# Operand-sum stores on SyncE's queue, weight sums spread over all gate steps, and another order of places at both ends of the down stage

## The chip, the cores and the metric

The kernel runs on one core of one Trainium2 chip. A core has TensorE (PE, the matmuls), VectorE (DVE), ScalarE (ACT), GpSimd (POOL) and SyncE (SP). Each has an instruction queue of its own that is worked off in order; SP issues DMAs only, and ACT issues DMAs between its own computations. The metric is the time of one execution on the device in microseconds, as the median of three runs; lower is better.

## What is computed

Two transformer-like blocks on 2048 tokens (and 16 meta tokens) with 1024 features. The change sits in the feed-forward part (FFN) of the first block, whose hidden size is 2816:

```
n2 = rmsnorm(h, norm2_g[i])
ff = jax.nn.silu(n2 @ w_gate[i]) * (n2 @ w_up[i])
h = h + ff @ w_down[i]
...
return second_block(first_block(...), ...)
```

Ahead of it the first block has a state-space mixer and a pooling mixer with an output projection; the second block has chunk-banded attention, gated linear attention and a gate on a per-layer embedding. Everything is float32 to the reference.

## The kernel before

**Precision.** Every float32 product is made of three matmuls of a rounded type: operand x is split into a high part (ACT copies it, `wh`, `xh`) and a low part (DVE or POOL subtracts the high part, `wl`, `xl`), and TensorE adds high by high, high by low and low by high. Splitting (`halves`, `split_in`) is thus work of ACT and of DVE or POOL for every operand.

**FFN.** The tokens are worked in two halves of 1024. For each half there is a gate stage (`gu_half`, `down_start` at its end) and a down stage (`down`). Both use a Strassen-like scheme: 2 by 2 blocks with 7 products in place of 8, so operands are sums and differences of blocks.

- *Gate stage*: 22 steps `j`, each of 7 products of 12 matmuls in the order 1, 2, 6, 5, 7, 3, 4 (line 1091). The operands of a step are made by `gu_w` (line 1033) one step ahead: `wr` (gate weights) and `wru` (up weights) are loaded, POOL and DVE make sums `wru`, `sq`, `wr`, and these are split into `wh`/`wl`, `wth`/`wtl`, `wsh`/`wsl`. ACT also takes the products out of PSUM (`t`, `raw`). Each pair of steps gives 7 hidden operands for the down stage: products in `raw`, `ha`, `hb`, `hc`, some with a POOL subtraction (`less`). `put` stores each to DRAM (`hd_d`): 77 stores of 256 KB in a half.
- *Weight sums*: 4 of the 7 left operands of the down stage are sums of blocks of `w_down`. `down_sums` (line 1186) makes them in gate half 0: 44 tiles, each with two loads (`sd<-in_w_down`), four POOL subtractions or additions of 128x128 (176 in all) and one store to `sd_d`. A step advances it twice.
- *Down stage*: 77 places of 12 matmuls (line 1316). `dn_load` loads the two operands, `dn_split` splits them: every third place (`dn_s % 3 == 1`) into the single tiles `wth`, `wtl`, `hc`, `hd`, the others into the doubly buffered `wh`, `wl`. The tile `hc` is the one that held a hidden operand in the gate stage. Place 0 and its loads begin inside the last gate step. Near the end of down half 0 (`n == 75`), `gu_prime` loads the first weights of gate half 1.

Beside this run background generators (`bg_step`): in gate half 0 `bias_table` (stores `eb_d<-e`, on ACT), in gate half 1 `norm` (stores `h_d<-nh`, on ACT).

**Order.** A framework takes the program text, and puts each engine's instructions into a queue order by priorities and data flow; semaphores do the rest. So the order on an engine can differ from the program text, and an instruction that waits holds back all that is behind it on its engine. `load` issues a DMA on SP, `store` on ACT:

```
def load(self, o, i):
    self.nc.sync.dma_start(out=o, in_=i)
def store(self, o, i):
    self.nc.scalar.dma_start(out=o, in_=i)
```

Of the kernel before, what the change touches and what calls it, by code (L numbers as in the profile page):

```python
# [10 lines left out]
ALU = mybir.AluOpType  # L11
# [24 lines left out]
class Build:  # L36
# [1034 lines left out]
        put(7, 4, *self.split_in(ru, self.wp, [128, KT, 128], 2, "", None))  # L1071
        yield 1

    def gu_prime(self):

        self.gu_js = [i // 2 + i % 2 * (NFF // 2) for i in range(NFF)]
        self.gu_raws = [self.gu_load(0, False), None]
        self.gw_steps = self.gu_w(0)
        next(self.gw_steps)

    def gu_half(self, half):

        def product(ps, p, first, last):
            hi, lo = w[p]
            x = self.xg[p]
            ks = range(4)
            for k in ks:
                for n, (l_, r_) in enumerate(((hi, 0), (hi, 1), (lo, 0))):  # L1090
                    self.pe.matmul(ps, lhsT=l_[:, k], rhs=x[k][r_], start=(first and k == n == 0),  # L1091
                                   stop=(k == 3 and n == 2), skip_group_check=True)

        def bank(name):
            return self.ps.tile([128, 512], F32, tag="ps", name=name, bufs=8)

        def gated(g):
            th = self.tmp("raw", 4)
            self.fn(th, g, AF.Tanh, scale=0.5)
            self.stt(th, th, 1.0, g, ALU.add, ALU.mult)  # L1100
            return th

        def keep(name):
            return self.fp.tile([128, 512], F32, tag=name, name=name, bufs=1)

        def less(o, x, y):
            self.tt(o, x, y, ALU.subtract, eng=self.pool)

        def put(p, x):
            self.store(self.hd_d[half, p - 1, jj], x)  # L1110

        sums = iter(()) if half else self.down_sums()
        for j in range(NFF):
            jj, late = j // 2, j % 2
            w = self.gw
            next(sums, None)
            nw = self.gu_w(j + 1) if j + 1 < NFF else iter(())
            pa, pb = bank("pa"), bank("pb")
            product(pa, 1, True, False)
            s1 = self.tmp("t", 2)  # L1120
            self.fn(s1, pa, AF.Copy)
            product(pb, 2, True, True)
            self.tt(s1, pb, s1, ALU.add)
            h0 = gated(s1)
            next(nw, None)
            next(nw, None)
            if j == NFF - 1:
                self.down_start(half)
                self.dn_load()
                self.dn_load()  # L1130
                self.dn_split()
            product(pa, 6, False, False)
            s2 = self.tmp("t", 2)
            self.fn(s2, pa, AF.Copy)
            pc = bank("pc")
            product(pc, 5, True, False)
            p5 = self.tmp("raw", 4)
            self.fn(p5, pc, AF.Copy)
            next(nw, None)
            product(pa, 7, False, False)  # L1140
            self.tt(p5, pa, p5, ALU.add)
            product(pc, 3, False, True)
            self.tt(s2, pc, s2, ALU.add)
            h1 = gated(s2)
            next(nw, None)

            if late:
                self.tt(h1, h1, p5, ALU.mult)
                put(3, h1)
                less(hb, h1, hb)  # L1150
                put(7, hb)
                less(hc, h1, hc)
                put(6, hc)
            else:
                hb = keep("hb")
                self.tt(hb, h1, p5, ALU.mult)
            next(sums, None)
            if j == 0 and self.r2_todo:
                self.mix_r2(*self.r2_todo.pop())
            if j % 2:  # L1160
                self.bg_step()
            product(pa, 4, False, True)
            if late:
                self.tt(h0, pa, h0, ALU.mult)
                put(2, h0)
                less(ha, h0, hc)
                put(4, ha)
            else:
                ha, hc = keep("ha"), keep("hc")
                self.tt(ha, pa, h0, ALU.mult)  # L1170
                put(1, ha)
                less(hc, hb, ha)
                put(5, hc)
            next(nw, None)
            self.bg_step()

# [9 lines left out]
    def down_sums(self):  # L1186

        wd, h = self.a["w_down"], NFF // 2

        def fetch(j, m):  # L1190
            t = self.fp.tile([128, 4, 128], F32, tag="ls", name="sd", bufs=3)
            self.load(t[:, 0:2], wd[j][:, m::4])
            self.load(t[:, 2:4], wd[j + h][:, m::4])
            return t

        todo = [(j, m) for j in range(h) for m in range(4)]
        nxt = fetch(*todo[0])
        for i, (j, m) in enumerate(todo):
            t = nxt
            if i + 1 < len(todo):  # L1200
                nxt = fetch(*todo[i + 1])
            for o, x, y, op in ((1, 0, 1, ALU.subtract), (3, 3, 1, ALU.subtract), (0, 0, 3, ALU.add), (2, 2, 3, ALU.subtract)):
                self.tt(t[:, o], t[:, x], t[:, y], op, eng=self.pool)
            self.store(self.sd_d[:, j, :, m * 128:(m + 1) * 128].rearrange("s p c -> p s c"), t)
            yield 1

    def down_start(self, half):
# [23 lines left out]
    def dn_split(self):  # L1231

        if not self.dn_raw or self.dn_s == len(self.dn):
            return
        w, x = self.dn_raw.pop(0)
        if self.dn_s % 3 == 1:
            wh, wl, xh, xl = (self.fp.tile([128, 512], F32R, tag=t, name=t, bufs=1) for t in ("wth", "wtl", "hc", "hd"))
        else:
            h, l_ = (self.wp.tile([128, 2, 512], F32R, tag=t, name=t, bufs=2) for t in ("wh", "wl"))
            wh, xh, wl, xl = h[:, 0], h[:, 1], l_[:, 0], l_[:, 1]  # L1240
        self.halves((wh, wl), w)
        self.halves((xh, xl), x)
        self.dn_s += 1
        self.dn_ops.append((wh, wl, xh, xl))

    def down(self, half):
# [9 lines left out]
        h1, kept, sums, hold, post = [], [[None] * KT for _ in range(2)], {}, {}, []  # L1256
# [35 lines left out]
        def done(p, m):  # L1292

            ps = (pa if p in (1, 6, 7, 4) else pb)[m]
            if p in (1, 6, 5):
                if m == 0:
                    places(p)
                self.fn(hold[p][m], ps, AF.Copy)
            elif p == 4:
                out(ps)  # L1300
            else:
                x = hold[{2: 1, 7: 5, 3: 6}[p]][m]
                self.tt(x, ps, x, ALU.add)
                out(x)
# [1 line left out]
        for _ in range(2):  # L1306
            fetch()
        for n, (p, j) in enumerate(self.dn):
            self.dn_split()
            self.dn_load()  # L1310
            wh, wl, xh, xl = self.dn_ops.pop(0)
            ps = pa if p in (1, 6, 7, 4) else pb
            for m in range(4):
                c = slice(m * 128, m * 128 + 128)
                for i, (l_, r_) in enumerate(((wh, xh), (wh, xl), (wl, xh))):
                    self.pe.matmul(ps[m], lhsT=l_[:, c], rhs=r_, start=(p in (1, 2, 5) and j == i == 0),
                                   stop=(j == NFF // 2 - 1 and i == 2), skip_group_check=True)
            if post:
                done(*post.pop(0))
            if j == NFF // 2 - 1:  # L1320
                post += [(p, m) for m in range(4)]
            if n % 4 == 1:
                self.bg_step()
            if n == 75:
                if half:
                    self.w_all = self.weights("proj")
                    self.w_next.append(self.get_w(0))
                else:
                    self.gu_prime()
                    next(self.gw_steps)  # L1330
        while post:
            done(*post.pop(0))
# [720 lines left out]
```

## Time and profile before

| | |
|---|---|
| Median of 3 runs | 3585.68 us (3585.02 to 3585.87) |
| The profiled execution | 3588.34 us, its span 3586.4 us |
| Mean granted TensorE clock | 0.957 |
| Busy, PE / DVE / ACT / POOL | 91% / 63% / 45% / 41% |
| DMA traffic | 573.95 MB, 160 GB/s |
| Gate half 0 / down half 0 | about 679 to 1146 us / 1157 to 1377 us |
| Gate half 1 / down half 1 | about 1377 to 1852 us / 1862 to 2078 us |

The span is the time between the first and the last instruction that the profiler saw; the time of an execution is a little longer. The granted clock is the share of full speed that TensorE was allowed. A busy share is an average over the whole span: a stage must be looked at by itself.

### The profile page before, as it was taken

What the parts mean: (1) busy time and instruction counts of PE and PEld (TensorE: products, weight loads), DVE (VectorE), ACT (ScalarE), POOL (GpSimd) and SP (SyncE); (2) the same over time, 40 slices, a digit from 0 to 9 for tenths busy, and PEclk for the clock granted to TensorE, in tenths of its full rate; (3) what the DMA queues carried; (4) which work ended last, traced back from release to release, by engine and by line L of the source; (5) the groups of instructions that cost most, each with busy time, mean ns of one, the idle gap of its engine ahead of it and who ended that gap; (6) DMA issues with size and microseconds to landing.
All of it is one profiled execution on the core that took longest, in us unless ns stands there. A gap on an engine that the chain in (4) does not pass through costs nothing. (4 is left out here: it accounts for less than half of the span.)

```text
span 3586.4 us, 46677 instructions
## 1 busy us (share of the span) xinstructions
PE 3273.8 (91%) x15874; PEld 2712.4 (76%) x15874; DVE 2253.7 (63%) x3697; ACT 1608.9 (45%) x2906; POOL 1469.1 (41%) x1234
## 2 busy tenths in 40 slices
PE   7897788789998998999989989999999999979897
PEld 7776666667887787777878777898888987867676
DVE  7776556754556756776555672335665446888774
ACT  5344533323333543344344442335665445766643
POOL 1265544798543203554520142232222235354534
PEclk8898899899999999999999999999999999989999
DMA  9634276676233664354356534565464565545341
GB/s 243 150 109 105 80 222 198 183 233 191 100 109 123 218 217 155 126 173 153 108 204 191 176 132 165 174 184 178 155 175 145 165 186 165 166 146 157 121 164 54
DMA packets 406342, 573.95 MB, mean 160 GB/s; under 512 B 90668, under 2 KB 222276, under 8 KB 406104
## 3 DMA queue, kind: packets, MB, share of 16 engines
q1 hardware_dynamic: 270144, 419.23, 39.7%
q10 hardware_dynamic: 135960, 151.75, 12.4%
q8 instruction: 125, 2.05, 0.2%
q14 instruction: 113, 0.93, 0.1%
HBM read 409.04 MB, written 151.71 MB: 156 GB/s over the span
## 5 line engine op out<-in xcount | busy, mean ns | idle before, releaser
L44 POOL TENSOR_TENSOR wl<-wr,wh 128x1024 fp32r<-128x1024 f32 (+1 forms) x147 | 372.7, 2537 | 314.7 <-ACT wh L54 295.2
L54 ACT ACTIVATE wh<-wr 128x1024 fp32r<-128x1024 f32 (+3 forms) x303 | 272.7, 902 | 341.6 <-PE pt L159 75.8
L158 PE MATMUL pt<-xh,wh 128*128 128x512 f32 x896 | 362.3, 405 | 16.3 <-ACT wh L54 8.2
L160 PE MATMUL pt<-xh,wl 128*128 128x512 f32 x896 | 358.8, 401 | 4.3 <-POOL wl L44 4.3
L159 PE MATMUL pt<-xl,wh 128*128 128x512 f32 x896 | 359.1, 401 | 0.2 <-DVE xl L44 0.2
L48 POOL TENSOR_SCALAR P<-P,rsm 128x640 f32<-128x640 f32 (+4 forms) x128 | 103.4, 808 | 346.7 <-DVE rsm L1628 285.2
L1091 PE MATMUL pa<-xh,wh 128*128 128x512 f32 x528 | 214.6, 407 | 24.2 <-ACT t L54 20.3
L44 DVE TENSOR_TENSOR wl<-wr,wh 128x512 fp32r<-128x512 f32 (+2 forms) x156 | 150.3, 964 | 106.0 <-ACT wh L54 105.6
L1091 PE MATMUL pa<-xh,wl 128*128 128x512 f32 x528 | 209.5, 402 | 3.7 <-POOL wl L44 3.6
L158 PEld LDWEIGHTS pt<-xh,wh 128*128 128x128 f32 x896 | 171.1, 191 | 54.3 <-ACT wh L54 9.6
L1091 PE MATMUL pa<-xl,wh 128*128 128x512 f32 x528 | 211.8, 401 | 0.0
L44 POOL TENSOR_TENSOR s<-s,sq 128x512 f32<-128x512 f32 x56 | 87.9, 1569 | 285.6 <-ACT sq L54 284.4
L160 PEld LDWEIGHTS pt<-xh,wl 128*128 128x128 f32 x896 | 170.7, 191 | 41.9 <-POOL wl L44 6.2
L159 PEld LDWEIGHTS pt<-xl,wh 128*128 128x128 f32 x896 | 171.3, 191 | 35.6 <-DVE xl L44 0.7
L1623 DVE CUSTOM_DVE_ANT_0 P<-s,bias 128x640 f32<-128x640 f32 (+4 forms) x128 | 94.6, 739 | 111.5 <-PE s L1618 71.2
L1488 PE MATMUL pv<-wh,xh 128*128 128x256 f32 (+1 forms) x512 | 148.0, 292 | 5.5 <-ACT wh L54 3.9
L1489 PE MATMUL pv<-wl,xh 128*128 128x256 f32 (+1 forms) x512 | 147.6, 289 | 0.7 <-POOL wl L44 0.7
L1490 PE MATMUL pv<-wh,xl 128*128 128x256 f32 (+1 forms) x512 | 147.0, 288 | 0.0
L1091 PE MATMUL pc<-xh,wsh 128*128 128x512 f32 x352 | 139.1, 395 | 6.0 <-ACT wsh L54 3.2
L1091 PEld LDWEIGHTS pa<-xh,wh 128*128 128x128 f32 x528 | 101.5, 192 | 54.2 <-ACT t L54 24.6
L54 ACT ACTIVATE wsh<-wr 128x1024 fp32r<-128x1024 f32 x44 | 46.6, 1060 | 211.9 <-PE pc L1091 149.8
L1091 PE MATMUL pc<-xl,wsh 128*128 128x512 f32 x352 | 139.0, 395 | 0.0
(516 smaller groups left out, 9898.2 us busy)
## 6 DMA issues: line engine op xcount, KB each, us to landing
raw<-hd_d SPq DMA_DIRECT2D x150, 256.0 KB, 3.6
wr<-in_w_out SPq DMA_DIRECT2D x56, 512.0 KB, 4.5
wr<-in_w_in SPq DMA_DIRECT2D x44, 512.0 KB, 3.8
wru<-in_w_up SPq DMA_DIRECT2D x44, 512.0 KB, 3.6
wr<-in_w_gate SPq DMA_DIRECT2D x44, 512.0 KB, 3.4
wr<-sd_d SPq DMA_DIRECT2D x88, 256.0 KB, 2.9
wr<-in_w_down SPq DMA_DIRECT2D x66, 256.0 KB, 3.7
nh<-h_d SPq DMA_DIRECT2D x64, 256.0 KB, 3.8
```

What stands on the lines that cost most here:

```text
L44: return (eng or self.dve).tensor_tensor(out=o, in0=x, in1=y, op=op)
L48: (eng or self.dve).tensor_scalar(out=o, in0=x, scalar1=s1, scalar2=s2, op0=op0, **kw)
L54: return self.act.activation(out=o, in_=x, func=func, **kw)
L158: self.pe.matmul(ps, lhsT=hi[k], rhs=xh[k], start=(first and k == 0), stop=False)
L159: self.pe.matmul(ps, lhsT=hi[k], rhs=xl[k], start=False, stop=False)
L160: self.pe.matmul(ps, lhsT=lo[k], rhs=xh[k], start=False, stop=(last and k == n - 1))
L1091: self.pe.matmul(ps, lhsT=l_[:, k], rhs=x[k][r_], start=(first and k == n == 0), stop=(k == 3 and n == 2), skip_group_check=True)
L1488: self.pe.matmul(pt, lhsT=xh, rhs=whi[:, k % 4], start=(k == 0), stop=False)
L1489: self.pe.matmul(pt, lhsT=xh, rhs=wlo[:, k % 4], start=False, stop=False)
L1490: self.pe.matmul(pt, lhsT=xl, rhs=whi[:, k % 4], start=False, stop=(k == KT - 1))
L1623: self.dve.tensor_tensor_reduce(out=v3(P[:, 0:w]), in0=sp[:, 0:np_, 0:n], in1=v3(bias[:, 640 - w:640]), scale=1.0, scalar=3e38, op0=ALU.ad ...
```

## The change

Three things, all in the FFN:

1. `put` and the store of `down_sums` go through `load`: 154 stores to `hd_d` and 44 to `sd_d` are issued by SP in place of ACT.
2. The two advances of `down_sums` move from two places inside a gate step to its end, and are placed after the step's last `less` on POOL, so that 8 of the 176 POOL operations fall in each of the 22 steps.
3. In the down stage the single tiles are taken at `dn_s % 3 == 2` (and at 73 and 76 near the end), `dn_split` and `dn_load` come behind a place's matmuls in the text; and at the end of down half 0 `gu_prime` loads both weights at `n == 73`, with the first three steps of `gu_w(0)` at 74, 75 and 76.

```
-    def gu_prime(self):
+    def gu_prime(self, both=False):
...
-        self.gu_raws = [self.gu_load(0, False), None]
+        self.gu_raws = [self.gu_load(0, False), self.gu_load(0, True) if both else None]
         self.gw_steps = self.gu_w(0)
-        next(self.gw_steps)
+        if not both:
+            next(self.gw_steps)
...
         def less(o, x, y):
-            self.tt(o, x, y, ALU.subtract, eng=self.pool)
+            self.less = self.tt(o, x, y, ALU.subtract, eng=self.pool)
 
         def put(p, x):
-            self.store(self.hd_d[half, p - 1, jj], x)
+            self.load(self.hd_d[half, p - 1, jj], x)
...
             w = self.gw
-            next(sums, None)
             nw = self.gu_w(j + 1) if j + 1 < NFF else iter(())
...
                 self.tt(hb, h1, p5, ALU.mult)
-            next(sums, None)
             if j == 0 and self.r2_todo:
...
                 put(5, hc)
+            with self.tc.issue_after(self.less.ins):
+                next(sums, None)
+                next(sums, None)
             next(nw, None)
...
-            self.store(self.sd_d[:, j, :, m * 128:(m + 1) * 128].rearrange("s p c -> p s c"), t)
+            self.load(self.sd_d[:, j, :, m * 128:(m + 1) * 128].rearrange("s p c -> p s c"), t)
...
-        if self.dn_s % 3 == 1:
+        if self.dn_s in (73, 76) or self.dn_s < 72 and self.dn_s % 3 == 2:
...
         for n, (p, j) in enumerate(self.dn):
-            self.dn_split()
-            self.dn_load()
             wh, wl, xh, xl = self.dn_ops.pop(0)
...
                                    stop=(j == NFF // 2 - 1 and i == 2), skip_group_check=True)
+            self.dn_split()
+            self.dn_load()
...
-            if n == 75:
-                if half:
-                    self.w_all = self.weights("proj")
-                    self.w_next.append(self.get_w(0))
+            if half and n == 75:
+                self.w_all = self.weights("proj")
+                self.w_next.append(self.get_w(0))
+            if not half and n >= 73:
+                if n == 73:
+                    self.gu_prime(True)
                 else:
-                    self.gu_prime()
                     next(self.gw_steps)
```

Three places show how the instructions move.

ACT in a gate step of half 0, from the split of the up weights (`wh<-wru`) to the split of the next operand (`wth<-sq`) and the product out of PSUM (`t<-pa`). Before:

```order
L54 ACTIVATE wh<-wru 128x1024
L54 ACTIVATE raw<-t 128x512
L54 ACTIVATE wh<-wr 128x1024
L60 DMA sd_d<-sd 128x4x128
L60 DMA hd_d<-ha 128x512
L60 DMA sd_d<-sd 128x4x128
L54 ACTIVATE wth<-sq 128x512
L54 ACTIVATE t<-pa 128x512
```

The same stretch of ACT's queue, of the changed kernel:

```order
L54 ACTIVATE wh<-wru 128x1024
L54 ACTIVATE wh<-wr 128x1024
L54 ACTIVATE raw<-t 128x512
L60 DMA eb_d<-e 128x256
L60 DMA eb_d<-e 128x512
L54 ACTIVATE wth<-sq 128x512
L54 ACTIVATE t<-pa 128x512
```

The stores of sums and of hidden operands no longer stand ahead of `wth` and `t`; the two of the bias table still do in the first steps.

TensorE from the last gate step (line 1091, in the changed kernel 1092) to the first places of the down stage (line 1316). Before, product 4 and then place 1, which is in the single tiles:

```order
L1091 MATMUL pa<-xh,wl 128x512
L1091 MATMUL pa<-xh,wh 128x512
L1091 MATMUL pa<-xl,wh 128x512
L1091 MATMUL pa<-xh,wl 128x512
L1316 MATMUL pa<-hc,wth 128x512 x4
```

Of the changed kernel, product 3, eleven matmuls of place 1, product 4 (its twelve, of which the inner ones read alike), the last of place 1, and place 2:

```order
L1092 MATMUL pc<-xl,wsh 128x512
L1092 MATMUL pc<-xh,wsl 128x512
L1316 MATMUL pa<-wh 128x512 x4
L1316 MATMUL pa<-wl,wh 128x512
...
L1316 MATMUL pa<-wl,wh 128x512
L1092 MATMUL pa<-xh,wh 128x512
...
L1092 MATMUL pa<-xh,wl 128x512
L1316 MATMUL pa<-wh,wl 128x512
L1316 MATMUL pa<-hc,wth 128x512 x4
```

Place 1 has moved ahead of product 4, and the first place in the tile `hc` is place 2.

DVE from down half 0 to gate half 1: `h` and `st` are the results of the down stage, `sq`, `wr` and `wtl` the operands of the first gate step. Before:

```order
L51 SCALAR_TENSOR_TENSOR h_11405<-pa,h_11405 128x512
...
L51 SCALAR_TENSOR_TENSOR st_10278<-h_11582,v_final_norm_g,st_10278 128x512
L44 TENSOR_TENSOR t<-pb,t 128x512
L51 SCALAR_TENSOR_TENSOR st_10278<-h_11590,v_final_norm_g,st_10278 128x512
L44 TENSOR_TENSOR sq<-wru 128x512
L51 SCALAR_TENSOR_TENSOR raw<-raw,t 128x512
L44 TENSOR_TENSOR wr<-wr,sq 128x512 x2
```

Of the changed kernel:

```order
L44 TENSOR_TENSOR wtl<-wr,wth 128x512
L44 TENSOR_TENSOR sq<-wru 128x512
L44 TENSOR_TENSOR wr<-wr,sq 128x512 x2
L51 SCALAR_TENSOR_TENSOR h_11403<-pa,h_11403 128x512
L51 SCALAR_TENSOR_TENSOR h_11436<-pa,h_11436 128x512
L51 SCALAR_TENSOR_TENSOR st_10278<-h_11403,v_final_norm_g,st_10278 128x512
L44 TENSOR_TENSOR wsl<-wr,wsh 128x1024
L44 TENSOR_TENSOR wtl<-sq,wth 128x512
```

`sq` and `wr` stood behind the four results of the down stage and now stand ahead of them.

## Rows read from the trace of the kernel before

**Rows 1.** The page: busy time, share of the span and instructions of each engine.

```profile
PE 3273.8 (91%) x15874; PEld 2712.4 (76%) x15874; DVE 2253.7 (63%) x3697; ACT 1608.9 (45%) x2906; POOL 1469.1 (41%) x1234
```

**Rows 2.** Stretches: us, busy PE, PEld, DVE, ACT, POOL (count), clock, DMA share, GB/s.

```profile
710.50:890.70 180.20, 162.91 (x674) 127.20 (x673) 92.97 (x111) 49.12 (x69) 158.38 (x184) 0.97 0.71 219
890.70:1124.00 233.30, 233.30 (x1009) 189.17 (x1008) 136.92 (x147) 80.65 (x112) 111.47 (x59) 1.00 0.29 101
...
1376.70:1410.90 34.20, 23.45 (x87) 17.74 (x86) 20.42 (x21) 10.58 (x16) 17.89 (x10) 0.80 0.23 77
1410.90:1610.20 199.30, 185.12 (x768) 146.18 (x767) 151.66 (x155) 82.22 (x115) 102.22 (x56) 0.97 0.44 147
1610.20:1829.80 219.60, 216.37 (x927) 174.75 (x926) 132.95 (x148) 83.61 (x116) 106.31 (x57) 0.99 0.36 124
```

**Rows 3.** PE's waits, 640 to 700: waiting instruction, releaser: us, times, longest.

```profile
PE mo L160 <- POOL wl L44: 4.5, 2, 2.6
PE pa L1091 <- DVE wtl L44: 3.8, 1, 3.8
```

**Rows 4.** PE's waits, 700 to 900.

```profile
PE pa L1091 <- ACT t L54: 11.6, 8, 7.9
```

**Rows 5.** Timeline of ACT in that stretch: start, us, instruction [idle before <-releaser].

```profile
765.84 0.38 ACTq L60 DMA_DIRECT2D sd_d<-sd  x1
...
771.27 0.63 ACT L54 ACTIVATE wth<-sq 128x512 fp32r<-128x512 f32 x1 [8.58 <-DMA sd_d<-sd]
```

**Rows 6.** ACT's waits, 700 to 900.

```profile
ACT t L54 <- POOL sd L44: 13.6, 4, 5.2
...
ACT raw L54 <- DVE e L1549: 6.3, 1, 6.3
```

**Rows 7.** Tile `sd`, POOL's instructions: ns min/median/max, first and last start.

```profile
L44 POOL TENSOR_TENSOR sd<-sd x176: 446/464/1457, 653.5 to 890.0; 128x128 f32<-128x128 f32 x176
```

**Rows 8.** Timeline of DVE, first gate step of half 0.

```profile
686.99 4.50 DVE L44 TENSOR_TENSOR wr<-wr,sq 128x512 f32<-128x512 f32 x2
```

**Rows 9.** PE's waits at the end of gate half 0, 1130 to 1160.

```profile
PE pa L1316 <- ACT hc L54: 10.3, 1, 10.3
```

**Rows 10.** PE's waits at the end of gate half 1, 1851 to 1900.

```profile
PE pa L1316 <- ACT hc L54: 9.9, 1, 9.9
```

**Rows 11.** Timeline of POOL at the end of gate half 0.

```profile
1147.81 1.71 POOL L44 TENSOR_TENSOR hc<-raw,hc 128x512 f32<-128x512 f32 x1
```

**Rows 12.** Timeline of ACT at the end of gate half 0.

```profile
1150.89 0.33 ACTq L60 DMA_DIRECT2D hd_d<-hc  x1
...
1156.04 0.63 ACT L54 ACTIVATE hc<-s 128x512 fp32r<-128x512 f32 x1 [0.75 <-DMA hd_d<-hc]
```

**Rows 13.** A stretch with the columns of rows 2, behind such a pause.

```profile
1862.10:1866.10 4.00, 4.00 (x9) 3.14 (x10) 0.66 (x1) 0.00 (x0) 0.00 (x0) 0.50 0.92 329
```

**Rows 14.** PE's waits at the start of gate half 1, 1380 to 1420.

```profile
PE pa L1091 <- ACT wth L54: 6.7, 1, 6.7
PE pc L1091 <- ACT wsh L54: 3.2, 1, 3.2
```

**Rows 15.** Timeline of DVE there.

```profile
1387.93 1.74 DVE L44 TENSOR_TENSOR sq<-wru 128x512 f32<-128x512 f32 x1
...
1394.77 0.68 DVE L44 TENSOR_TENSOR wr<-wr,sq 128x512 f32<-128x512 f32 x1
```

**Rows 16.** PE's waits in gate half 1, 1420 to 1650.

```profile
PE pa L1091 <- ACT t L54: 11.4, 5, 4.4
```

**Rows 17.** Timeline of ACT in gate half 1, one step.

```profile
1442.68 0.60 ACT L54 ACTIVATE t<-pa 128x512 f32<-128x512 f32 x1 [4.68 <-DVE nh L51]
```

**Rows 18.** The same, another step.

```profile
1490.73 0.63 ACT L54 ACTIVATE wth<-sq 128x512 fp32r<-128x512 f32 x1 [3.86 <-POOL ha L44]
```

**Rows 19.** Timeline of SP in a steady gate step of half 0.

```profile
950.90 0.33 SPq L57 DMA_DIRECT2D wr<-in_w_gate  x1
```

**Rows 20.** Timeline of ACT, the step behind it.

```profile
974.04 1.06 ACT L54 ACTIVATE wh<-wr 128x1024 fp32r<-128x1024 f32 x1 [1.08 <-PE pb L1091]
```

**Rows 21.** The page: DMA issues, their KB and median us to landing.

```profile
wr<-in_w_gate SPq DMA_DIRECT2D x44, 512.0 KB, 3.4
```

## The prediction

> **What bounds the kernel now.** The page comes first: TensorE is busy 91% of the span, the next engine 63% [rows 1]. So almost any gain must come out of TensorE's pauses, and the question is where those are. The table of stretches tells. In steps 9 to 21 of gate half 0 TensorE is busy for all of 233.3 us: 12 steps, so a step without pauses takes 233.3 / 12 = 19.44 us. The same code needs 180.2 us for steps 1 to 8, 34.2 us for step 0 of half 1, 199.3 us for its steps 1 to 9, and 219.6 us for its steps 10 to 20 [rows 2]. The excess over 19.44 us a step is 24.7, 14.8, 24.3 and 5.8 us. In the first of these stretches POOL is busy 158 of 180 us, in the pauseless one 111 of 233: the sums are all worked off early, up to 890 us [rows 7], when the weights' own low parts are also due on POOL.
>
> The views of waits say who ends the pauses. In gate half 0 it is nearly always the copy of a product out of PSUM, `t`, on ACT [rows 4]. ACT is not short of time there (49 of 180 us busy) [rows 2], it stands. The timeline shows how: the store of a weight sum is at the head of ACT's queue, the split `wth` behind it starts after 8.58 us of standing [rows 5], then `t` runs, and TensorE has waited 7.9 us, the longest wait of that group [rows 4]. A store's issue takes 0.4 us; what costs is that it waits on ACT for POOL's result. ACT's own list of waits agrees: `t` 13.6 us behind POOL's `sd` [rows 6].
>
> **The change, part by part.** I number the terms; the sum goes against the profiled execution (3588.34 us), which is 2.7 us above the median of the runs.
>
> 1. *End of the mixer stage and gate step 0.* POOL's sums stood between low parts of weights; TensorE waited 4.5 us for POOL's `wl` and 3.8 us for `wtl` [rows 3]. In front of `wtl` two DVE operations took 4.50 us [rows 8], where one such takes 0.68 [rows 15]: 3.1 us over, beside POOL's sums. The new order has no sum on POOL before the first step's last subtraction. So 4.5 + 3.1, and about 0.9 us of clock (below): **8.5 us**. Bounds 4 (only half of the waits go) and 11 (all of both, with the clock).
>
> 2. *Steps 1 to 8 of half 0*, excess 24.7 us. With neither sums nor hidden operands stored on ACT, what is left there are the stores of the bias table, which wait for DVE's `e` and hold ACT in the first steps: 6.3 us in one row [rows 6]. I keep 5 us for these: **19.7 us**. Bounds 12 (the bias table holds as long twice over) and 24 (all).
>
> 3. *Gate to down, both halves.* TensorE waits 10.3 and 9.9 us for the split `hc` [rows 9, 10]: place 1 is to be split into the tile `hc`, whose hidden operand is made by POOL until 1147.81 + 1.71 = 1149.5, sent from ACT only at 1150.9 and landed at about 1155.3 (1156.04 less the 0.75 of standing); the split runs at 1156.0 [rows 11, 12]. Now place 1 is in other tiles, and its 12 matmuls (12 x 19.44 / 84 = 2.8 us) run before product 4; place 2 is the one that waits. The store can go when POOL is done, so about 1.4 us earlier. 2.8 + 1.4, and a little of the clock: 4.5 us a half, **9 us**. Bounds 6 and 13.
>
> 4. *Down half 0 to gate half 1*, excess 14.8 us. TensorE waits 6.7 us for `wth` and 3.2 us for `wsh` [rows 14]; `wth` needs DVE's `sq`, which runs at 1387.9 behind all results of the down stage [rows 15]. With the weights fetched two places earlier and `sq`, `wr` ahead of those results, both waits should go, and with them clock: **11 us**; 3.8 us stay, for the results' own loads and copies. Bounds 7 and 13.5.
>
> 5. *Steps 1 to 20 of half 1*, excess 24.3 + 5.8 = 30 us. Its waits are for `t` again [rows 16], but of two kinds. In one ACT stands behind a hidden operand's store (3.86 us behind POOL's `ha`) [rows 18]; in the other behind the background norm (4.68 us behind DVE's `nh`) [rows 17], whose stores stay on ACT. By following each long pause back I put a third down to the first kind, half to the second: **10 us** go. Bounds 5 and 13.
>
> 6. *New costs.* Work is moved, not added. The 176 sums (0.464 us each) [rows 7] now fall 8 to a step, 3.7 us of POOL in 19.44 us where POOL is under half busy [rows 2]; the 198 issues on SP, at 0.4 us, are 4 us a step on an engine that does nothing else. From DVE's 4.50 us [rows 8] I take some delay in steps 9 to 21, and the changed rotation of tiles in the down stages is worth nothing to TensorE in either direction that I can see: **-3 us**, bounds -20 (1.5 us in each of 13 steps) and +5.
>
> *The clock* is in the terms: behind a long pause the granted clock is 0.50 for 4 us (1.2 in place of 2.4 GHz) [rows 13], while in a pauseless stretch it is 1.00. Such a spell is 2 us of lost work at most, and goes with the pause.
>
> Sum: 8.5 + 19.7 + 9 + 11 + 10 - 3 = 55.2 us. 3588.3 - 55.2 = 3533.1, less 2.7: **3531 us**. All terms at their upper bounds (74.5 us) give 3511; all at their lower ones (34 - 20 = 14) give 3572.
>
> A rule speaks against terms 2 and 5. The Trainium skill, "DMA: Bandwidth & Descriptors", section "Issuing engines are not separate DMA queues", says that DMAs of all engines run on the same 16 DMA engines, and that another issuing engine saves only the sequencer's time to initiate. Read with 0.4 us for an issue, it makes the move to SP worth little, which is rival A; the 8.58 us [rows 5] speak against this reading, since the sequencer also stands while a store's data isn't ready.
>
> **The rivals.**
>
> *A: the move to SP is worth its issue time only*, because the data or the DMA engines, not ACT's queue, set the pace. Then terms 2 and 5 together give what ten pauses lose in issue, 4 us, and term 3 loses the 1.4 us a half: 8.5 + 4 + 6.5 + 11 - 3 = 27 us, 3559 us. For it: DMA share 0.71 in steps 1 to 8 [rows 2]. Against it: ACT standing behind `sd`, not behind landings [rows 6].
>
> *B: new waits take half.* Where ACT no longer stands for sums it stands for the bias table's and the norm's stores [rows 6, 17], and POOL's sums meet DVE's sums of two tiles [rows 8]. Terms 2, 3, 4, 5 at 10, 4.5, 6 and 3: 8.5 + 23.5 - 3 = 29 us, 3557 us. For it: both kinds of store stay on ACT. The Trainium skill, "SBUF — State Buffer", section "Who interferes with whom", has DVE with two inputs in SBUF and a reading POOL instruction exclude each other; rows 8 agree (4.50 us for two).
>
> *C: slower, through SP's queue.* SP works in order too. A store of a sum now waits at its head for POOL, and the next weights' loads stand behind it. In a steady step the gate weights are sent for at 950.9 and land 3.4 us later, and ACT splits them at 974.0 [rows 19 to 21]: 23.1 - 3.4 = 19.7 us to spare. If SP is held for longer than that in a step, each step waits for a landing: 3.4 us and 2 us of clock, 5.4 us in 18 steps (22 less the first four, whose loads were sent before the stores), 97 us, against 55 gained: 3588.3 + 42 - 2.7 = 3628 us. Against it: a whole step's length is spare, and the sums of a step need only 3.7 us of POOL and come last in it.
>
> **How the numbers follow.** A measurement of this kernel tells about 0.2% (7 us) from no change. The forecast has 0.57, A 0.10, B 0.21, C 0.12. Faster: all of the forecast, 0.09 of A and 0.18 of B, 0.84. Within 0.2%: the weak ends of A, B and C, 0.01, 0.03 and 0.02, 0.06. Slower: 0.10 of C. The range from 3510 to 3572 takes in the sum's bounds, and A and B with them; what is left out is C, some of the edges of the others, 0.2 in all.
>
> **What would show it.** Right: in steps 1 to 8 of half 0 ACT no longer stands behind `sd` or a store of `sd_d`, and the stretch is near 160 us; steps 9 to 21 keep 19.4 to 19.7 us with POOL busier; the pause before the first place in `hc` is 5 to 6 us, not 10; gate step 0 of half 1 takes about 23 us; the waits behind `nh` stay. Wrong: pauses for `wh` or `wl` whose releaser is a landing of `wr` or `wru` (C); steps 9 to 21 longer than 20 us with DVE operations of several us (B); waits for `t` of the old size behind `e` (B), or steps 1 to 8 as long as before though ACT has no stores of sums (A).

## The result, and the profile after

The changed kernel takes 3551.95 us (median of 4 runs, 3551.42 to 3554.38) where the kernel before takes 3585.77 (4 runs): ratio 0.9907, 95% interval 0.9891 to 0.9922. That is 34 us faster, inside the range, where 3531 us was forecast. The direction and most of the places were right; two terms of the sum (1 and 3) brought next to nothing, and the term that brought most (2) did so by another cause than the one given.

The page's busy times of the changed kernel, in the columns of [rows 1]:

```profile
PE 3272.3 (92%) x15874; PEld 2717.1 (76%) x15874; DVE 2268.4 (64%) x3697; ACT 1612.7 (45%) x2906; POOL 1483.5 (42%) x1234
```

TensorE's work is the same; what changed is its pauses, and the clock behind them. The stretches of the changed kernel, in the columns of [rows 2]: steps 1 to 8 of half 0, steps 9 to 20, step 21 with down half 0, step 0 of half 1, its steps 1 to 20, and step 21 with down half 1:

```profile
709.95:873.29 163.34, 157.64 (x673) 127.35 (x672) 103.61 (x112) 55.62 (x75) 114.20 (x104) 0.98 0.55 171
873.30:1106.20 232.90, 232.90 (x1010) 189.30 (x1009) 147.30 (x145) 80.07 (x110) 167.97 (x155) 1.00 0.50 154
1106.17:1361.22 255.05, 238.50 (x1010) 192.15 (x1009) 178.38 (x251) 120.86 (x213) 63.42 (x42) 0.97 0.69 221
1361.22:1382.71 21.49, 19.96 (x86) 15.62 (x85) 19.70 (x19) 8.05 (x13) 14.50 (x8) 1.00 0.39 123
1382.71:1794.32 411.61, 399.27 (x1694) 320.36 (x1692) 284.02 (x306) 167.44 (x233) 212.35 (x113) 0.98 0.40 137
1794.32:2040.38 246.06, 235.77 (x1011) 191.48 (x1010) 152.64 (x220) 116.28 (x203) 31.78 (x17) 0.98 0.64 205
```

The same stretches of the kernel before, where [rows 2] cut them otherwise:

```profile
1124.04:1376.82 252.78, 236.30 (x1009) 192.36 (x1008) 176.62 (x252) 120.74 (x213) 50.12 (x25) 0.97 0.67 215
1410.89:1829.85 418.96, 401.55 (x1694) 320.93 (x1693) 284.66 (x302) 165.88 (x230) 208.54 (x113) 0.98 0.40 135
1829.85:2078.14 248.29, 235.66 (x1011) 191.06 (x1010) 154.28 (x220) 116.75 (x203) 27.82 (x17) 0.97 0.63 203
```

The gain is in steps 1 to 8 (180.2 to 163.3 us, with POOL's share down from 158 of 180 us to 114 of 163) and in step 0 of half 1 (34.1 to 21.5, where the clock stays at 1.00 in place of 0.80). The stretch with the start of down half 0, where a gain was forecast, is 2.3 us longer.

The table sets all kernels of this study side by side, in us, from the starts of the first matmul of each step in the one profiled execution of each. "To step 1" is all that lies ahead of step 1 of half 0, "rest" all behind the down stage of half 1. "Rotation" is the choice of the places that are split into the single tiles, with the order of splits that goes with it. Runs of one kernel, measured together, spread by 3 to 16 us (before: 3574 to 3589 in one such group). Stretches of the same code mostly differ by up to 4 us between profiles, once by 7.5 (steps 1 to 20 of half 1: 419.0 us before, 411.5 with the early fetch alone), so a single difference of that size shows nothing.

| Kernel | to step 1 | 1 to 8 | 9 to 20 | 21, down 0 | 0 of half 1 | 1 to 20 | 21, down 1 | rest | ratio to before (95%) |
|---|---|---|---|---|---|---|---|---|---|
| before | 710.5 | 180.2 | 233.4 | 252.8 | 34.1 | 419.0 | 248.3 | 1508.2 | 1 |
| changed | 709.9 | 163.3 | 232.9 | 255.0 | 21.5 | 411.6 | 246.1 | 1512.0 | 0.9907 (0.9891 to 0.9922) |
| changed, second time | 707.1 | 163.4 | 232.9 | 255.5 | 21.8 | 411.6 | 243.8 | 1510.3 | 0.9919 (0.9899 to 0.9938) |
| stores alone | 712.4 | 180.9 | 233.4 | 246.2 | 34.0 | 411.6 | 249.6 | 1500.7 | 0.9989 (0.9978 to 1.0) |
| sums alone | 707.2 | 163.5 | 232.9 | 251.8 | 33.4 | 415.4 | 246.4 | 1506.7 | 0.9944 (0.9925 to 0.9963) |
| places and fetch alone | 712.1 | 179.7 | 233.4 | 252.2 | 21.5 | 413.5 | 245.8 | 1501.7 | 0.9950 (0.9932 to 0.9967) |
| early fetch alone | 711.6 | 181.0 | 233.4 | 251.5 | 24.9 | 411.5 | 248.9 | 1511.0 | 0.9981 (0.9972 to 0.9991) |
| changed, stores on ACT | 708.7 | 163.6 | 232.9 | 255.1 | 21.4 | 413.6 | 248.6 | 1507.7 | 0.9919 (0.9904 to 0.9933) |
| changed, table's stores on SP | 708.1 | 165.4 | 232.9 | 254.0 | 23.0 | 409.6 | 243.9 | 1508.1 | 0.9915 (0.9896 to 0.9934) |
| changed, no sums in step 21 | 709.5 | 163.2 | 232.9 | 252.8 | 23.3 | 409.4 | 246.1 | 1512.3 | 0.9914 (0.9899 to 0.9929) |
| changed, old rotation | 706.2 | 163.2 | 232.9 | 250.4 | 21.9 | 410.7 | 249.6 | 1500.5 | 0.9888 (0.9873 to 0.9902) |
| changed, table's load ahead | 712.2 | 163.7 | 232.9 | 255.1 | 21.4 | 411.9 | 244.6 | 1511.0 | 0.9905 (0.9889 to 0.9922) |
| the last, with old rotation and no sums in step 21 | 710.3 | 163.3 | 232.9 | 250.3 | 22.4 | 411.5 | 251.1 | 1511.8 | 0.9903 (0.9884 to 0.9921) |
| changed, rotation by half | 708.2 | 163.3 | 232.9 | 252.0 | 23.4 | 410.1 | 243.5 | 1513.7 | 0.9912 (0.9898 to 0.9927) |

### The profile page after: what moved, and what is told of

Its sections match the earlier page's. It is cut to its first block, busy times and chain, and to the rows that moved or that the text cites. A ratio compares the mean times of both kernels' runs of the same rounds, so it can differ in the third digit from the quotient of the medians.

```text
span 3552.4 us, 46642 instructions
## 1 busy us (share of the span) xinstructions
PE 3272.3 (92%) x15874; PEld 2717.1 (76%) x15874; DVE 2268.4 (64%) x3697; ACT 1612.7 (45%) x2906; POOL 1483.5 (42%) x1234
## 4 chain that ended last, share of the span: by engine, by line
PE 37%; DVE 7%; DMA 5%; ACT 3%; issue 3%; POOL 1%; ACTq 0%; SPq 0%; DVEq 0%; POOLq 0%
PE pt L158 4%; PE pt L160 4%; PE pt L159 4%; PE pa L1316 3%; PE pa L1092 3%; PE pb L1316 2%; PE pv L1663 2%; PE pc L1092 1%; PE s L1621 1%; PE pv L1492 1%; PE pv L1493 1%; PE tp L1647 1%; PE pv L1491 1%; PE pg L158 1%; DMA raw<-mix_d 1%
## 5 line engine op out<-in xcount | busy, mean ns | idle before, releaser
L1092 PE MATMUL pc<-xh,wsl 128*128 128x512 f32 x352 | 138.1, 392 | 1.2 <-DVE wsl L44 1.2
```

## The experiments

### Each part of the change alone

Stores alone: the kernel before with

```
-            self.store(self.hd_d[half, p - 1, jj], x)
+            self.load(self.hd_d[half, p - 1, jj], x)
...
-            self.store(self.sd_d[:, j, :, m * 128:(m + 1) * 128].rearrange("s p c -> p s c"), t)
+            self.load(self.sd_d[:, j, :, m * 128:(m + 1) * 128].rearrange("s p c -> p s c"), t)
```

> Only the 198 stores move to SyncE; the sums stay early, the places as before. Standing theory (ACT stands behind stores whose data POOL hasn't made): steps 1 to 8 of gate half 0 fall from 180 us to 163 to 170 although the sums are as early as before, gate half 1 loses some 7 us of pauses, its step 0 stays at 34 us; in all 3555 to 3566 us. Issue theory (rival A, a move saves only the issue): steps 1 to 8 at 176 or more, in all 3578 to 3585. Queue theory (rival C): SyncE stands for the early sums with the weights behind it, pauses for wh or wl, 3590 or more.

Measured 0.9989 (3577.9 us): my theory of ACT's standing fails, the issue theory's time holds. Steps 1 to 8 take 180.9 us as before. TensorE's waits there, 700 to 900, show why:

```profile
PE pa L1091 <- POOL wl L44: 11.4, 5, 4.2
PE pc L1091 <- ACT raw L54: 4.8, 2, 3.7
```

The wait for `t`, 11.6 us before [rows 4], is gone; in its place TensorE waits 11.4 us for low parts of weights, which were 1.1 us before. ACT's timeline and then POOL's, ahead of the longest of these:

```profile
827.88 1.07 ACT L54 ACTIVATE wh<-wru 128x1024 fp32r<-128x1024 f32 x1 [1.25 <-POOL sd L44]
```

```profile
831.93 4.51 POOL L44 TENSOR_TENSOR sd<-sd 128x128 f32<-128x128 f32 x8 [0.53 <-DMA sd<-in_w_down]
836.39 1.28 POOL L44 TENSOR_TENSOR hb<-raw,hb 128x512 f32<-128x512 f32 x1
837.62 1.26 POOL L44 TENSOR_TENSOR hc<-raw,hc 128x512 f32<-128x512 f32 x1
838.84 2.34 POOL L44 TENSOR_TENSOR wl<-wru,wh 128x1024 fp32r<-128x1024 f32 x1
```

The high part `wh`, all that `wl` still needed, was there at 828.95; `wl` ran at 838.84, behind eight sums in a row and two subtractions. With or without ACT standing, POOL had some 156 to 158 us of work in 180, in an order that put the sums first. Standing was the last of two delays with one source, and taking it away showed the other. SyncE now did the standing, 49.6 us of it for sums in this stretch, and TensorE had no wait for a landing there:

```profile
SPq L57 <- POOL sd L44: 49.6, 28, 7.3
```

Sums alone: the kernel before with the two advances of `down_sums` at the step's end, behind the last `less`:

```
-            next(sums, None)
...
+            with self.tc.issue_after(self.less.ins):
+                next(sums, None)
+                next(sums, None)
```

> Only the sums are spread over the 22 steps; all stores stay on ACT, the places as before. Standing theory: ACT still stands behind sums in every step, so that steps 1 to 8 gain little (over 172 us) and steps 9 to 21 get pauses they did not have (over 236 us for twelve); in all 3575 to 3600 us. Crowding theory (POOL's early crowd of sums was the cost, not ACT's standing): steps 1 to 8 at 160 to 168, steps 9 to 21 as before, in all 3565 to 3572.

Measured 0.9944 (3560.7 us): steps 1 to 8 take 163.5 us, as the crowding theory has it, though every store is on ACT, and steps 9 to 20 lose nothing. The total is 4 us better than that theory's.

Places and fetch alone: everything of the third part, the rest as before.

> Only the order of places and the earlier fetch at the end of down half 0; sums early and stores on ACT as before. If the late sums in step 21 took back the gain at the start of down half 0 (theory): with POOL free there, the excess from the last gate step to the end of down half 0 falls from 22.6 us to 14 to 19, step 0 of gate half 1 from 34 to 22 us; in all 3563 to 3570 us. If the new rotation itself makes the second wait (for hd behind hc): that wait of some 3 us is here too, the excess stays at 21 to 24, and only step 0 of half 1 gains; in all 3571 to 3576.

Measured 0.9950 (3563.1 us). The second wait, for `hd`, is here too (2.6 us) with no sums near it, and the stretch of down half 0 stays at 252.2: the rival's place. Step 0 of half 1 falls to 21.5. The total beat the rival's, by more than these stretches explain (below, "rest").

The early fetch alone:

```
-        self.gu_raws = [self.gu_load(0, False), None]
+        self.gu_raws = [self.gu_load(0, False), self.gu_load(0, True) if both else None]
...
+            if not half and n >= 73:
+                if n == 73:
+                    self.gu_prime(True)
```

> The kernel before with one part of the third change alone: at the end of down half 0 both weights are fetched at place 73 and the first operands made at 74 to 76; the places' rotation, the sums and the stores as before. Theory (this part alone carries the gain at the start of gate half 1): step 0 there falls from 34.1 to 21 to 24 us and the rest stays, in all 10 to 13 us under the kernel before. Rival (the new rotation is needed, since its tiles come free earlier): step 0 stays over 28 us, in all within 6 us of before.

Measured 0.9981, 7 us under the kernel before, less than the 10 to 13 expected; step 0 of half 1 takes 24.9 us, a little over its 21 to 24. So the fetch brings 9.2 of the 12.6 us without the other parts. The new rotation is not needed for the rest: the changed kernel with the old one takes 21.9 us there.

### What the stores' move is worth beside the others

The changed kernel with `put` and the store of `down_sums` back on ACT (the first diff, reversed).

> The changed kernel with all 198 stores back on ACT: sums spread, new places. New theory (the early crowd of sums on POOL was the cost; ACT standing behind their stores only showed it): steps 1 to 8 of half 0 stay at 162 to 166 us and steps 9 to 20 at 233; only the hidden operands' stores stand in ACT's way, 3 to 8 us in gate half 1 and about 1 to 2 us at each gate to down; in all 4 to 10 us over the changed kernel on the same chip. Old theory (standing on ACT is a cost of its own): steps 1 to 8 at 172 or more, in all 15 us or more over the changed kernel.

Measured 0.9919 as the changed kernel on the same chip (0.9919): nothing to be told in the total, less than the 4 to 10 us expected. Steps 1 to 8 take 163.6 us, so all four pairings have been run: with early sums 180.2 us (stores on ACT) and 180.9 (on SyncE), with spread sums 163.6 and 163.3. What is seen is one place, the start of down half 1, where TensorE's wait, 1810 to 1850, is

```profile
PE pa L1316 <- ACT hc L54: 11.0, 1, 11.0
```

and in the changed kernel, 1816 to 1850,

```profile
PE pa L1316 <- ACT hc L54: 7.9, 1, 7.9
```

(6.9 us in its second profile), 3 to 4 us less. The profiles of all kernels show that this takes both parts, the move and the new rotation. The wait for `hc` at the start of down half 1:

| | stores on ACT | stores on SyncE |
|---|---|---|
| old rotation | 9.3 to 10.9 us (3 profiles) | 11.7 to 12.1 (3) |
| new rotation | 10.6 and 11.0 (2) | 6.6 to 7.9 (6) |

At the start of down half 0 the new rotation shortens it by itself: 9.5 to 10.7 us with the old rotation, 6.0 and 6.1 with the new one and stores on ACT, 5.2 to 5.9 on SyncE. Why the move makes the wait longer with the old rotation stays open.

The changed kernel itself was run again, as a base:

> The changed kernel itself on the same chip, to be the base of the other three: 0.990 to 0.993 of the kernel before by every theory; its stretches should come within 2 us of those of its first profile where nothing but the run differs.

It came to 0.9919, its stretches within 2.8 us of the first profile, where 2 were expected.

### The pause that came new: the bias table

In the changed kernel step 1 of half 0 takes 27.5 us where it took 21.3. The pause came with the spread sums: step 1 takes 27.6 us with the sums alone, 19.4 with the stores alone and 21.5 with places and fetch alone. The timeline of ACT in the changed kernel:

```profile
725.54 0.33 ACTq L60 DMA_DIRECT2D eb_d<-e  x1
725.97 0.63 ACT L54 ACTIVATE wth<-sq 128x512 fp32r<-128x512 f32 x1 [3.84 <-DVE e L48]
726.99 0.33 ACTq L60 DMA_DIRECT2D eb_d<-e  x1
727.42 0.60 ACT L54 ACTIVATE t<-pa 128x512 f32<-128x512 f32 x1 [0.82 <-DVE e L1552]
```

and TensorE's waits from 700 to 900, all of them:

```profile
PE pa L1092 <- ACT t L54: 5.7, 1, 5.7
```

Two edits were tried. The stores on SyncE:

```
-            self.store(c[:, 0:512], f)
-            self.store(c[:, 512:768], e[:, 1:257])
+            self.load(c[:, 0:512], f)
+            self.load(c[:, 512:768], e[:, 1:257])
```

> The changed kernel with the bias table's 16 stores on SyncE too. Theory (the pause of 5.7 us in step 1 comes of ACT standing behind these stores, with 1.9 us of clock behind it): step 1 of half 0 falls from 27.5 to 19.5 to 21 us, in all 6 to 8 us under the changed kernel. Rival (DVE itself stands for the loads of e, which are late, so products stay in PSUM all the same): step 1 stays over 24 us, in all within 3 us.

Step 1 fell to 19.6 us as expected, but steps 2 to 8 rose from 135.9 to 145.8; the ratio is 0.9915. TensorE's waits from 730 to 890:

```profile
PE pa L1092 <- DVE raw L44: 6.6, 2, 5.4
```

DVE stood twice, the second time for a load, and what it owed TensorE stood behind:

```profile
751.78 0.75 DVE L51 SCALAR_TENSOR_TENSOR nh<-nh,v_norm_g,r 128x512 f32<-128x512 f32 x1 [1.86 <-issue]
753.51 0.75 DVE L51 SCALAR_TENSOR_TENSOR nh<-nh,v_norm_g,r 128x512 f32<-128x512 f32 x1 [0.99 <-DMA nh<-h_d]
...
754.78 0.68 DVE L44 TENSOR_TENSOR raw<-pa,raw 128x512 f32<-128x512 f32 x1
```

That load had left late, behind the table's stores on SyncE, which stood there until `e` was made:

```profile
743.47 0.43 SPq L57 DMA_DIRECT2D wru<-in_w_up  x1
746.51 0.32 SPq L57 DMA_DIRECT2D eb_d<-e  x1
746.92 0.38 SPq L57 DMA_DIRECT2D hd_d<-ha  x1
747.39 3.41 SPq L57 DMA_DIRECT2D nh<-h_d  x2
```

This is rival C's mechanism, once. Steps 2 to 8 are 10 us longer with it; that the stores are what delayed `nh`, and that this is the whole price, is read from the order of the queue and not shown by a run.

The table's load one background step ahead of its use:

```
             self.load(e[:, 0:257], self.a["rel_rev"][:, h])
+            yield 1
```

> The changed kernel with the bias table's load issued one background step ahead of its use; its stores stay on ACT. Theory (the pause in step 1 comes of ACT standing behind stores whose data is late because DVE stands for the load): step 1 of half 0 falls from 27.5 to 19.5 to 22 us and no later step takes it up, steps 2 to 8 stay at 136; in all 5 to 8 us under the changed kernel. Rival (the wait only moves, as with the stores on SyncE): steps 1 to 8 together stay over 161 us.

Nothing changed (step 1 at 27.8, 0.9905): DVE still stood 3.6 us for the load of `e`. The edit moves the program text; the load left SyncE no earlier (10.6 us into step 1 in both kernels). How to get rid of this pause stays open.

### The start of the down stage

The changed kernel's waits at the start of down half 0, 1110 to 1145:

```profile
PE pa L1316 <- ACT hc L54: 5.9, 1, 5.9
PE pa L1316 <- DVE hd L44: 3.6, 1, 3.6
```

`hc` is as forecast (10.3 less 4.5). Behind it comes `hd`, the low part of the same operand, and DVE's timeline tells what stands ahead of that:

```profile
1137.66 3.43 DVE L44 TENSOR_TENSOR xl<-t,xh 128x512 fp32r<-128x512 f32 x2
1141.01 0.94 DVE L44 TENSOR_TENSOR wl<-raw,wh 128x512 fp32r<-128x512 f32 x1
1141.87 0.94 DVE L44 TENSOR_TENSOR hd<-raw,hc 128x512 fp32r<-128x512 f32 x1
```

No sums in the last step, two tiles more in earlier ones:

```
-                next(sums, None)
-                next(sums, None)
+                for _ in range(0 if j == NFF - 1 else 3 if j in (10, 15) else 2):
+                    next(sums, None)
```

> The changed kernel with no sums in the last gate step of half 0: two more tiles are made in steps 10 and 15 instead. Theory (the wait of 3.6 us for hd, behind the one for hc, comes of DVE meeting these last eight sums on POOL): that wait falls under 1 us, the stretch from step 21 to the end of down half 0 from 255.0 to 249 to 252 us, steps 9 to 20 stay at 233. Rival (the new rotation or the loads make it): the stretch stays over 253.5.

The wait for `hd` is 3.3 us all the same: the sums of the last step are not its cause. That the slow pair of `xl` ahead of `hd` is the cause is read from DVE's order; no run took it away. At the start of down half 1, where there is no wait for `hd`, DVE makes `xl` too, but singly and, right ahead of `hd`, with POOL idle:

```profile
1825.61 0.68 DVE L44 TENSOR_TENSOR xl<-nh,xh 128x512 fp32r<-128x512 f32 x1
1827.36 0.69 DVE L44 TENSOR_TENSOR hd<-raw,hc 128x512 fp32r<-128x512 f32 x1 [1.07 <-ACT hc L54]
```

The stretch (252.8) is between what the two expected, within the scatter.

The old rotation, and the old order of split and matmuls, in the changed kernel:

```
-        if self.dn_s in (73, 76) or self.dn_s < 72 and self.dn_s % 3 == 2:
+        if self.dn_s % 3 == 1:
...
+            self.dn_split()
+            self.dn_load()
             wh, wl, xh, xl = self.dn_ops.pop(0)
...
-            self.dn_split()
-            self.dn_load()
```

> The changed kernel with the old rotation of the down stage's tiles (single tiles at place 1) and the old order of split and matmuls; sums spread, stores on SyncE and the early fetch stay. Theory (the new rotation only turns one wait of 9 to 10 us for hc into two, for hc and hd, and adds one for wl): the stretch from step 21 to the end of down half 0 comes to 246 to 253 us where the changed kernel has 255, in all 0 to 8 us under the changed kernel. Rival (the rotation does save its 4.5 us a half): 257 to 260 us, and 2 to 9 us over it in all.

250.4 us in half 0, 4.7 less than with the new rotation; half 1 takes 249.6, 3.5 to 5.8 more. The ratio 0.9888 is the best of all, but its interval meets that of the changed kernel run again, and 10 us of it lie in "rest".

All three edits together:

> The changed kernel with three edits at once: old rotation, no sums in step 21, the bias table's load one step ahead. If the three add up: step 1 at 19.5 to 22, step 21 and down half 0 at 246 to 252 us, in all 3536 to 3546 where the changed kernel has 3550. If waits take each other's place: over 3547.

0.9903 (3548.7 us): the gains do not add up. The stretch of half 0 takes 250.3 us, as with the old rotation; step 1 keeps its pause.

Last, the rotation by half, old in half 0 and new in half 1 (`self.dn_s % 3 == 1 + self.dn_half`, and the split ahead of or behind the matmuls likewise):

> The changed kernel with the old rotation and order of splits in down half 0 and the new one in down half 1. Theory (in half 0 the low parts of the next half's activations on DVE make the second place's low part late, so the new rotation gains nothing there; in half 1 there are none, and it gains): step 21 and down half 0 take 249 to 252 us as with the old rotation (changed kernel 255), step 21 and down half 1 take 243 to 247 as with the new one (old rotation 249.6); in all 0.986 to 0.990 of the kernel before, some 5 to 9 us under the changed kernel. Rival (half 1's shorter pause was the runs' scatter): half 1 at 248 to 251, the whole no better than the kernel with the old rotation in both halves or the changed kernel.

Stage by stage the theory's times held: 252.0 us in half 0, with waits from 1110 to 1145 much as they were before,

```profile
PE pa L1319 <- ACT hc L54: 10.3, 1, 10.3
PE pa L1319 <- DVE hd L44: 1.0, 1, 1.0
```

and 243.5 us in half 1. The theory's reason does not hold as it was put: half 1 has low parts `xl` on DVE as well, and what differs is how they fall, as shown above. And the whole is 0.9912 where 0.986 to 0.990 was expected, no better than the changed kernel, with 1513.7 us in "rest". So the 3 to 6 us saved in these stretches are not seen in the total, and no version is shown to beat the changed kernel.

## Why the prediction was right or wrong

*The total* lay in the range, 21 us above the forecast; rival B's 3557 us came nearer. Against the profiled execution the terms were to give 55.2 us; the spans differ by 34.0. Term by term, from the table:

1. *End of the mixer stage and step 0*, 8.5 us forecast: 0.6 (3.3 in the second profile). The step that failed is that in front of `wtl` two DVE operations took 4.50 us "beside POOL's sums". The trace of the kernel before already shows otherwise: while they ran (686.99 to 691.42), POOL was mostly at low parts, `xl` up to 688.2 and then

```profile
688.16 2.78 POOL L44 TENSOR_TENSOR wl<-wru,wh 128x1024 fp32r<-128x1024 f32 x1
690.91 0.90 POOL L44 TENSOR_TENSOR sd<-sd 128x128 f32<-128x128 f32 x1
```

   The sums are gone, and DVE's operations are still slow beside the same low parts. POOL and DVE in the first gate step of the changed kernel:

```profile
686.36 2.82 POOL L44 TENSOR_TENSOR wl<-wru,wh 128x1024 fp32r<-128x1024 f32 x1
```

```profile
686.88 2.85 DVE L44 TENSOR_TENSOR sq<-wru 128x512 f32<-128x512 f32 x1
```

   `sq` lasts as long as the POOL instruction beside it. The waits for `wl` and `wtl` from 640 to 700 shrank, 8.3 to 5.0 us, and others grew by about as much: 1.5 us for a further `wl`, 0.5 for `t`, 1.0 for a split `sq` on ACT.
2. *Steps 1 to 8*, 19.7 forecast: 16.8. The cause was wrong, and that the size came near is luck. I gave it to the stores' move; the stores alone bring nothing there, the sums alone all of it, and the changed kernel with its stores on ACT keeps it. What of the sum was mis-sized is the bias table: 5 us kept, 8 lost in step 1 with the clock (27.5 less 19.4).
3. *Gate to down*, 9 forecast: 0 in all, 2.3 lost in half 0 and 2.2 gained in half 1 (4.5 in the second profile). The step that failed is that behind `hc` nothing else was late. In half 0 the wait for `hc` shrank as worked out (10.3 to 5.9), but behind it came one of 3.6 us for the low part `hd`, which stands on DVE behind the low parts of the next half's activations (that these are its cause is argued from the order). TensorE's idle time in the stretch is 16.5 us before and 16.6 after, and the other 2.2 us lie in its busy time. A wait of 4.2 us for `wl` some places on is not new, the kernel before has one of 4.3 for `hd` there. In half 1 it shrank by 2 to 3 us only (9.9 to 7.9 and 6.9).
4. *Down half 0 to half 1*, 11 forecast: 12.6. Right, and shown: the fetch alone brings 9.2, and the kernels with other parts of the change beside it take 21.4 to 23.4 us, with the new rotation or the old.
5. *Half 1, steps 1 to 20*, 10 forecast: 7.4. Mostly not shown to come of the stores. The five profiles with stores on ACT have 411.5 to 419.0 us here (middle 413.6), the nine with stores on SyncE 409.4 to 411.9 (middle 411.5). Before's one profile, 419.0, is the highest of all; from middle to middle the stores are worth some 2 us.
6. *New costs*, -3 forecast: steps 9 to 20 lost nothing (0.5 us won) with POOL at 168 of 233 us, so the sums' 8 a step are covered by TensorE's work, as reasoned. "Rest" lost 3.8. It runs from 1500.5 to 1513.7 us in the kernels of the table, whose second block is the same code in slightly other orders; the cause isn't settled.

The sum, 0.6 + 16.8 + 0 + 12.6 + 7.4 + 0.5 - 3.8 = 34.1, is the spans' difference within rounding.

*Slips in the working* that move no forecast: the pauseless stretch is steps 9 to 20, which are the 12 steps, not 9 to 21. The sum of the upper bounds leaves term 6 at nothing; with its +5 it is 3506 us, outside the range. SyncE's new issues are 5.5 a step in half 0 (77 and 44 in 22 steps), some 2 us and not 4. In rival A term 3 less 1.4 us a half is 6.2, not 6.5.

*The rivals.* A, that the move to SyncE is worth its issue time only, had 0.10 and was right about the move, wrong about the time, since the sums' spreading brought what I had charged to the move. The Trainium skill's rule, "DMA: Bandwidth & Descriptors", section "Issuing engines are not separate DMA queues", that another issuing engine saves only the initiating time, agrees with the total of the kernel with its stores on ACT (0.9919 and 0.9919). The one place where the runs show more is the start of down half 1, 3 to 4 us with the new rotation. B, new waits in the place of the old, is what terms 3 and 2 met (`hd`, the bias table), though not by the norm's stores or by the sums. C did not come with the change: SyncE stood 47.5 us for sums in steps 1 to 8 of the changed kernel, and TensorE's one wait there was for `t`; it came once, with the table's stores.

## What to carry to other kernels

The releaser that a view names for a wait can be the last of several; ask what else is late by the same source. Here ACT stood behind stores because POOL's queue held background sums ahead of work that was due, and moving the stores only handed the wait to POOL. So look for the engine that is full in the stretch (POOL, 158 of 180 us) and spread its background work by where it stands in the queue, before moving the instructions that wait for it. When a wait is shortened by moving one operand, check the second operand of the same matmuls, and the queue of the engine that makes it.

## What the runs showed that was not expected

Two things. A DVE addition or subtraction of two tiles of 128x512 took 0.68 us [rows 15] and, beside a POOL instruction of 2.82 us, 2.85 us: it began 0.52 us behind that and ended 0.55 us behind it. So the first gate step was as slow for DVE with the sums gone, since the POOL instructions beside it were the weights' low parts. The Trainium skill, "SBUF — State Buffer", section "Who interferes with whom", says that a DVE instruction with two SBUF inputs contends with a GpSimd instruction that reads SBUF, over ports that are an exclusive lock; these rows agree. And in the kernel with the stores alone SyncE could stand 49.6 us of a 200 us stretch for stores whose data was late, without TensorE waiting for a landing of the weights behind them. Gate weights had time to spare there (sent for at 808.54, split at 829.97); up weights had less, and POOL waited for one landing, 1.4 us.
